# Hybrid decoder step on one core: the place of the constants' small operations and of the first cached-key loads

## The chip, the core and the metric

The kernel runs on one core of a Trainium2 chip. A core has a matrix engine (TensorE, PE in the profile; PEld is its weight load), a vector engine (VectorE, DVE), an engine for activation functions (ScalarE, ACT), a general one (GpSimd, POOL) and an engine that here only starts transfers (SyncE, SP). Each works through its own queue in order; they wait for each other by semaphores. Transfers between the chip's large memory and the core's memory run on 16 DMA engines, started from the queues of SyncE, ScalarE and GpSimd. The metric is the device time of one execution in microseconds. The kernel before took 1861.91 us in the median of three runs (1861.57 to 1862.14).

## The reference

One decoder layer for a prompt of 256 positions and 8 samples of one position each, with the same weights:

```
q, k, v, z, xbc, dt, qm, gates = in_proj(rmsnorm(x))      # one 2048 x 13856 projection
A = sliding-window attention(q, k, v)                     # window 128, ALiBi, sinks
B = SSD scan(xbc, z, dt)                                  # depthwise conv, chunked scan, gated norm
M = cross attention(qm, memory keys, memory values)       # 4 heads of 256, 256 memory tokens
x = x + W_out(g_A * P_A(A) + g_B * P_B(B) + g_M * P_M(M))
x = x + swiglu(rmsnorm(x))
```

For the prompt the memory's keys and values are computed (`w_mem_kv`), for the samples they come from a cache: `cache_mem_k` and `cache_mem_v`, 8 samples x 256 tokens x 1024 values. Everything is fp32; the caches and states are outputs too.

## The kernel before

All features lie along the 128 partitions, and the 264 positions (256 of the prompt and 8 samples) along the columns. The weights are streamed. A **unit** is one block `raw` of 128 x 1024 weights (512 KB), and each unit goes the same way: SyncE loads it (line 261, four buffers); ScalarE rounds it to `hi` (line 183); VectorE takes the rest, `lo = raw - hi` (line 184); TensorE multiplies by `hi` and `lo` (line 162). `hi` and `lo` have three buffers each, so `hi` of unit n waits until TensorE is done with unit n-3, and a block's load waits until VectorE is done with the block four before.

Units 0 to 31 are the memory stage (`mem_group`, accumulators `pmem`): four groups of 8 units, 12 matmuls of 512 columns each; groups 0 and 1 give the keys (norm at line 458), groups 2 and 3 the values. Units 32 to 47 are the projection of the prompt's and samples' memory queries (`qm`, accumulators `pin`), 24 matmuls of 264 columns each, and further groups of `pin` follow; behind them the branches, the output projection and the feed-forward part.

All other work is cut into small steps in generators. `Side.step` runs some of them after each unit, and `side.drain(name)` runs the list up to the end of a named one. The list begins with `mem_norm` ("m"), `prep_x` ("x", the normed activations as `hh` and `hl`: line 578 and the split at lines 183 and 184), `consts` ("c"), `dt_work` ("D"), `mem_keys`, `mem_prompt_work`. The part `consts` makes small tables: slopes and sinks (lines 663 to 675), masks (676 to 679), `na_bc = -exp(a_log)` on 128 x 32 (lines 680 and 681), the same for one column `hcol` (682 and 683), and from the convolution's state, through six transposes, `pre` (lines 688 to 695). Their inputs are loaded by SyncE behind the blocks 17 to 23. `before_q` calls `side.drain("c")` ahead of unit 32. `dt_work` sums `hh` and `hl` to `xf` (line 602).

`mem_prompt_work` squares and transposes the queries; the samples' queries are written to memory as `qd` (line 819, GpSimd's queue). `mem_sample_work` reads each sample's row of `qd` back, broadcast to 128 partitions, as `qb` (line 870), and multiplies it with the cached keys on VectorE (line 875). The cached keys come through `memk_loads` (line 738, GpSimd's queue), a generator that keeps three tiles ahead of the reader.

The order of the instructions on each engine is not the order of the program text: a scheduler at build time puts every instruction where its engine and its inputs are free by its own clock, unless an edge holds it. `tc.issue_after(i)` puts such an edge: each instruction made inside the block stands in its own engine's queue behind `i`, if `i` is on the same engine. It is an order within a queue and no wait for another engine. `state["split_at"]` is the last `hi` that was made (ScalarE), `state["rest_at"]` the last `lo` (VectorE).

Of the kernel before, what the change touches and what calls it, by code (L numbers as in the profile page):

```python
# [79 lines left out]
def tile_hybrid_decoder_step(  # L80
# [9 lines left out]
    nc = tc.nc  # L90
# [9 lines left out]
    side = Side()  # L100
# [7 lines left out]
    def half(name, dt=F32):  # L108
        return ap_.tile([P, 8, NT], dt, tag="A", name=nm(name))

    def t4(name, dt=F32):
        return tp.tile([P, 4 * NT], dt, tag="t4", name=nm(name), bufs=4)
# [4 lines left out]
    def const(shape, name, dt=F32, tag=None):  # L117
        return cp.tile(shape, dt, tag=tag or name, name=name)
# [29 lines left out]
    def t1(name, dt=F32):  # L148
        return tp.tile([P, NT], dt, tag="t1", name=nm(name), bufs=4)

    def tiny(name, n):
        assert n <= 64
        return tp.tile([P, 64], F32, tag="tiny", name=nm(name), bufs=9)[:, 0:n]
# [4 lines left out]
    def sps(name):  # L158
        return pq.tile([P, 512], F32, tag="s", name=nm(name))
# [4 lines left out]
    def tr(out, in_):  # L164
        n = in_.shape[0]
        return nc.tensor.transpose(out, in_, ident[0:n, 0:n])  # L166
# [84 lines left out]
    state = dict(dma=0, split=0)  # L251
# [456 lines left out]
    qt = {}  # L708

    def before_q():  # L710
        side.drain("c")
        qt["qm"] = half("qmT")

    def after_copy(dst):
# [5 lines left out]
    mT = {}  # L720
# [10 lines left out]
    def ahead(sources, pool, depth):  # L731
        tiles = []
        for n in range(len(sources)):
            while len(tiles) < min(n + (depth() if callable(depth) else depth), len(sources)):
                b, src = sources[len(tiles)]
                t = pool("ld")
                for to, of in src(t) if callable(src) else ((t.rearrange("p (b c) -> p b c", b=b) if b else t, src),):
                    nc.gpsimd.dma_start(to, of)
                tiles.append(t)
            yield tiles[n]  # L740
# [8 lines left out]
    def anywhere(name):  # L749
# [3 lines left out]
    memk_loads, memv_loads = (  # L753
        ahead([(None, c[0, b, mc * P:(mc + 1) * P].rearrange("m h d -> m (h d)")) for b in range(NS) for mc in range(2)],
              pool, depth) for c, pool, depth in ((cache_mem_k, anywhere, 3),
                                   (cache_mem_v, values_home, lambda: 3 if ring_free[0] else 2)))
# [15 lines left out]
    def mem_prompt_work():  # L772
# [42 lines left out]
        qrow = t1("qrow")[0:64, 0:P]  # L815
        V.tensor_copy(qrow, p2[0:64, 0:P])
        qd = dr.tile([NS, 1024], F32, name="qd")
        for d in range(2):
            nc.gpsimd.dma_start(qd.rearrange("b (h d c) -> d b h c", h=4, d=2)[d], qrow[32 * d:32 * d + 32])
        mT["qd"] = qd  # L820
        yield 1.5

        for hp in range(2):
            den = tiny("den", 4)
            pT = [t2("pT").rearrange("p (mc t) -> p mc t", mc=2) for _ in range(2)]
            for tb in range(2):
                ps = sps("scm").rearrange("p (h m) -> p h m", h=2)
                for h in range(2):
                    for d in range(2):
                        c = 2 * (2 * hp + h) + d  # L830
# [33 lines left out]
    def mem_sample_work():  # L864
        rq, qd = mT["rq"], mT["qd"]

        sc = const([P, 64], "scs", tag="pTs").rearrange("p (mc b h) -> p mc b h", mc=2, b=NS)
        for b in range(NS):
            qb = t4("qb")[:, 0:1024]
            nc.gpsimd.dma_start(qb, qd[b:b + 1].broadcast_to([P, 1024]))  # L870
            for mc in range(2):
                kc = next(memk_loads)
                jk = t1("jks")
                for h in range(4):
                    V.tensor_tensor_reduce(jk[:, 0:256], kc[:, h * 256:(h + 1) * 256], qb[:, h * 256:(h + 1) * 256],
                                           1.0, 0.0, ALU.mult, ALU.add, sc[:, mc, b, h:h + 1])
                yield 2.0
        ps = sps("sct")
        for mc in range(2):
            tr(ps[0:32, mc * P:(mc + 1) * P], sc[:, mc].rearrange("p b h -> p (b h)"))  # L880
        mx = tiny("mxs", 2)[0:32]
        V.tensor_reduce(mx[:, 0:1], ps[0:32, 0:256], axis=AX.X, op=ALU.max)
        V.tensor_tensor(mx[:, 0:1], mx[:, 0:1], rq[0:32, 17:18], op=ALU.mult)
        pm = t1("pms")[0:32, 0:256]
        act(pm, ps[0:32, 0:256], AF.Exp, scale=rq[0:32, 8:9], bias=mx[:, 0:1], accum_out=mx[:, 1:2])
        V.reciprocal(mx[:, 1:2], mx[:, 1:2])
        V.tensor_scalar(pm, pm, mx[:, 1:2], None, op0=ALU.mult)
        ps = sps("pst")
        for mc in range(2):
            tr(ps[:, mc * 32:(mc + 1) * 32], pm[:, mc * P:(mc + 1) * P])  # L890
        pT = const([P, 64], "pTs")
        V.tensor_copy(pT, ps[:, 0:64])
        mT["p"] = pT
        yield 1.5
# [952 lines left out]
    side.add("D", dt_work(), ["dtw"])  # L1847
    side.add("Km", mem_keys(), ["keys"])
    side.add("Mp", mem_prompt_work(), ["qm"])
    slow.add("Mk", mem_sample_work(), ["q"])  # L1850
    slow.add("Ms", mem_sample_values())
    side.add("W1", swa_keys(), ["kv"])
# [15 lines left out]
    with tc.issue_after(first["load1"].ins):  # L1868
        h = act(warm[:, 0:1], warm[:, 0:1], AF.Copy)
# [65 lines left out]
```

## Time and profile before

| | |
|---|---|
| median of three runs | 1861.91 us |
| the profiled execution's own time | 1862.31 us |
| its span, first to last instruction | 1860.6 us |
| TensorE's granted clock over the span | 1.000 |
| first `pmem` matmul, first `pin` matmul | 8.15 us, 105.91 us |
| VectorE busy from 100 to 110 us, from 110 to 120 us | 10.00 us, 9.39 us |
| DMA, mean over the span | 218 GB/s |

The times in the views are microseconds from the start of the span. The rows of a timeline give the start, the duration, the engine, the line, the operation with its output and inputs and a count; in brackets stands how long the engine was idle before the row, and what it then had waited for. Durations of matmuls overlap, so the distance between two starts tells more than the duration.

### The profile page before, as it was taken

What the parts mean: (1) busy time and instruction counts of PE and PEld (TensorE: products, weight loads), DVE (VectorE), ACT (ScalarE), POOL (GpSimd) and SP (SyncE); (2) the same over time, 40 slices, a digit from 0 to 9 for tenths busy, and PEclk for the clock granted to TensorE, in tenths of its full rate; (3) what the DMA queues carried; (4) which work ended last, traced back from release to release, by engine and by line L of the source; (5) the groups of instructions that cost most, each with busy time, mean ns of one, the idle gap of its engine ahead of it and who ended that gap; (6) DMA issues with size and microseconds to landing.
All of it is one profiled execution on the core that took longest, in us unless ns stands there. A gap on an engine that the chain in (4) does not pass through costs nothing.

```text
span 1860.6 us, 37257 instructions
## 1 busy us (share of the span) xinstructions
PE 1853.2 (100%) x15062; PEld 1810.6 (97%) x15062; DVE 1209.4 (65%) x2355; ACT 953.7 (51%) x1402; POOL 152.7 (8%) x299
## 2 busy tenths in 40 slices
PE   9999999999999999999999999999999999999999
PEld 7789999998999999999999999999999999999999
DVE  6776578776788878887455675555445555445555
ACT  6555466665777676764444444444334443334442
POOL 1100002101011111110000001000000000100001
PEclk9999999999999999999999999999999999999999
DMA  9986669677778777787888767656766556865565
GB/s 282 295 236 201 207 226 300 210 247 235 240 229 264 236 242 243 246 253 241 231 230 253 182 198 219 185 184 179 184 184 183 184 184 180 230 209 182 183 190 150
DMA packets 210265, 406.36 MB, mean 218 GB/s; under 512 B 29487, under 2 KB 34494, under 8 KB 210084
## 3 DMA queue, kind: packets, MB, share of 16 engines
q1 hardware_dynamic: 181508, 323.52, 58.9%
q0 software_dynamic: 21776, 74.15, 12.0%
q10 hardware_dynamic: 6808, 6.30, 1.1%
q8 instruction: 118, 1.93, 0.4%
q14 instruction: 55, 0.45, 0.1%
HBM read 378.38 MB, written 27.81 MB: 218 GB/s over the span
## 4 chain that ended last, share of the span: by engine, by line
PE 61%; DVE 0%; issue 0%; ACT 0%
PE pdn L162 14%; PE pg L162 14%; PE pu L162 14%; PE pin L162 7%; PE pout L162 5%; PE pus L162 5%; PE pua L162 3%; PE py L162 0%; DVE lo L184 0%; PE pst L162 0%; DVE ring L1515 0%; DVE y L1474 0%; PE xtok L166 0%; PE ssy L162 0%; PE yt L166 0%; PE cb L162 0%
## 5 line engine op out<-in xcount | busy, mean ns | idle before, releaser
L184 DVE TENSOR_TENSOR lo<-raw,hi 128x1024 fp32r<-128x1024 f32 (+1 forms) x651 | 747.2, 1153 | 538.4 <-ACT hi L183 535.9
L183 ACT ACTIVATE hi<-raw 128x1024 fp32r<-128x1024 f32 (+1 forms) x651 | 648.1, 1003 | 812.2 <-PE pin L162 184.3
L162 PE MATMUL pin<-hl,hi 128*128 128x264 f32 x1728 | 486.3, 284 | 0.0
L162 PE MATMUL pin<-hh,hi 128*128 128x264 f32 x1728 | 485.5, 284 | 0.0
L162 PE MATMUL pin<-hh,lo 128*128 128x264 f32 x1728 | 474.8, 283 | 0.1
L162 PEld LDWEIGHTS pin<-hl,hi 128*128 128x128 f32 x1728 | 324.2, 188 | 4.2 <-issue 4.0
L162 PEld LDWEIGHTS pin<-hh,hi 128*128 128x128 f32 x1728 | 323.8, 188 | 3.8 <-issue 2.9
L162 PEld LDWEIGHTS pin<-hh,lo 128*128 128x128 f32 x1728 | 318.2, 188 | 3.7 <-issue 3.1
L162 PE MATMUL pu<-h2l,hi 128*128 128x264 f32 x704 | 197.8, 282 | 0.0
L162 PE MATMUL pdn<-fal,hi 128*128 128x264 f32 x704 | 197.7, 282 | 0.0
L162 PE MATMUL pu<-h2h,hi 128*128 128x264 f32 x704 | 197.7, 282 | 0.0
L162 PE MATMUL pg<-h2l,hi 128*128 128x264 f32 x704 | 197.7, 283 | 0.0
L162 PE MATMUL pdn<-fah,hi 128*128 128x264 f32 x704 | 197.3, 282 | 0.0
L162 PE MATMUL pg<-h2h,hi 128*128 128x264 f32 x704 | 197.0, 282 | 0.0
L162 PE MATMUL pdn<-fah,lo 128*128 128x264 f32 x704 | 194.8, 282 | 0.0
L162 PE MATMUL pu<-h2h,lo 128*128 128x264 f32 x704 | 194.7, 282 | 0.0
L162 PE MATMUL pg<-h2h,lo 128*128 128x264 f32 x704 | 194.4, 282 | 0.0
L162 PEld LDWEIGHTS pdn<-fal,hi 128*128 128x128 f32 x704 | 132.0, 188 | 0.0
L162 PEld LDWEIGHTS pg<-h2l,hi 128*128 128x128 f32 x704 | 132.0, 187 | 0.0
L162 PEld LDWEIGHTS pg<-h2h,hi 128*128 128x128 f32 x704 | 132.0, 187 | 0.0
L162 PEld LDWEIGHTS pu<-h2l,hi 128*128 128x128 f32 x704 | 132.0, 187 | 0.0
L162 PEld LDWEIGHTS pu<-h2h,hi 128*128 128x128 f32 x704 | 131.9, 187 | 0.0
(527 smaller groups left out, 2940.4 us busy)
## 6 DMA issues: line engine op xcount, KB each, us to landing
raw<-in_w_in_dram SPq DMA_DIRECT2D x216, 512.0 KB, 4.5
raw<-in_w_gate_dram SPq DMA_DIRECT2D x88, 512.0 KB, 3.6
raw<-in_w_up_dram SPq DMA_DIRECT2D x88, 512.0 KB, 3.5
raw<-in_w_down_dram SPq DMA_DIRECT2D x88, 512.0 KB, 5.0
raw<-in_w_up_ssd_dram SPq DMA_DIRECT2D x32, 512.0 KB, 6.4
raw<-in_w_out_dram SPq DMA_DIRECT2D x32, 512.0 KB, 5.1
raw<-in_w_mem_kv_dram SPq DMA_DIRECT2D x31, 512.0 KB, 6.5
ring<-in_state_ssm_dram POOLq DMA_DIRECT2D x32, 256.0 KB, 5.1
```

The costliest lines, as they stand in the source:

```text
L162: return nc.tensor.matmul(out, lhsT=lhsT, rhs=rhs, start=start, stop=stop)
L183: h = act(hi, src, AF.Copy)
L184: return h, V.tensor_tensor(lo, src, hi.bitcast(F32), op=ALU.subtract)
```

## The change

The instructions of `consts` that are made in `before_q` get their place behind the newest `hi` on ScalarE and behind the newest `lo` on VectorE, which are those of unit 35. That holds for all that the drain runs at that time, so also for the last steps of `prep_x`, the activations. Key loads are placed behind the store of `qd` on GpSimd's queue. Nothing is computed otherwise, and no buffer changes.

```diff
     def before_q():
-        side.drain("c")
+        with tc.issue_after(state["split_at"].ins), tc.issue_after(state["rest_at"].ins):
+            side.drain("c")
         qt["qm"] = half("qmT")
...
         for d in range(2):
-            nc.gpsimd.dma_start(qd.rearrange("b (h d c) -> d b h c", h=4, d=2)[d], qrow[32 * d:32 * d + 32])
+            mT["qd_at"] = nc.gpsimd.dma_start(qd.rearrange("b (h d c) -> d b h c", h=4, d=2)[d], qrow[32 * d:32 * d + 32])
...
             for mc in range(2):
-                kc = next(memk_loads)
+                with tc.issue_after(mT["qd_at"].ins):
+                    kc = next(memk_loads)
```

SyncE's queue is the same as before. On ScalarE the difference begins in the memory stage, at units 15 and 16; `hi_606` and `hi_626` are the `hi` of these units, and line 554 squares the rows of the prompt:

```order
 L183 ACTIVATE hi_606<-raw_581 128x2x512
 L554 ACTIVATE jkx_522,ssx_523<-x_321 128x512 x2
-L680 ACTIVATE na_bc<-na_bc 128x32
 L183 ACTIVATE hi_626<-raw_601 128x2x512
 L554 ACTIVATE jkx_522,ssx_523<-x_483 128x512
```

Line 680 no longer stands ahead of the `hi` of unit 16; line 682, two units further, is gone from there too, and both now stand behind the `hi` of unit 35.

On VectorE the operations of lines 666 to 683 stood around the `lo` of units 15 to 26 (and lines 676 to 679 at the start of the program). The new place is behind `lo_1132`, the `lo` of unit 35; `xn` are the scaled activations:

```order
 L184 TENSOR_TENSOR lo_1132<-raw_1099,hi_1131 128x1024
+L578 SCALAR_TENSOR_TENSOR xn_1135<-xr_550,vgc,rb_924 128x264
+L578 SCALAR_TENSOR_TENSOR xn_1139<-xr_550,vgc,rb_924 128x264
+L666 TENSOR_SCALAR pack<-pack 128x16
+L669 TENSOR_TENSOR m_214_1211<-ident 128x64
+L676 MEMSET pack 128x62
+L679 TENSOR_REDUCE jm<-ident 32x16
+L681 TENSOR_SCALAR na_bc<-na_bc 128x32
+L184 TENSOR_TENSOR hl_123<-xn_1125,hh_121 128x264
+L683 TENSOR_SCALAR hcol<-hcol 32x1
+L693 TENSOR_TENSOR tm_1235<-scT_1231,cw 128x288
```

These rows now stand together there; lines 670, 677 and 678 follow ahead of the `lo` of unit 37, lines 674 and 675 ahead of those of units 38 and 39, and lines 693 and 695 have moved from units 33 and 34 to units 36 and 37. On TensorE the transposes of the convolution's state stand in three places (units 27, 29 and 30) instead of two (28 and 31), and in units 36 to 38 products with `hi` go ahead of those with `lo`.

On GpSimd's queue, before, around the store of `qd` (`ld_` and `ring` are tiles for cached keys, `vm` the prompt's memory values; the other three key loads stand further ahead):

```order
L440 DMA out_dram<-vm_117 128x512 x2
L738 DMA ld_2387<-in_cache_mem_k_dram 128x1024
L440 DMA out_dram<-vm_117 128x512 x2
L655 IOTA ti_1152 128x256
L657 AFFINE_SELECT nd<-nd 128x256
L659 AFFINE_SELECT nd<-nd 128x256
L819 DMA qd<-qrow_1926 32x128 x2
L870 DMA qb_2382<-qd 128x1024
L870 DMA qb_2462<-qd 128x1024
```

And in the changed kernel, whose later lines have numbers higher by one:

```order
L440 DMA out_dram<-vm_117 128x512 x4
L655 IOTA ti_1152 128x256
L657 AFFINE_SELECT nd<-nd 128x256
L659 AFFINE_SELECT nd<-nd 128x256
L820 DMA qd<-qrow_1926 32x128 x2
L739 DMA ld_2384<-in_cache_mem_k_dram 128x1024
L739 DMA ring<-in_cache_mem_k_dram 128x1024
L739 DMA ld_2387<-in_cache_mem_k_dram 128x1024
L739 DMA ring<-in_cache_mem_k_dram 128x1024
L871 DMA qb_2382<-qd 128x1024
```

All four early key loads now stand between the store of `qd` and the four loads of `qb`.

## The prediction

> **What bounds the kernel now.** I read the page's busy table first, then the timeline of TensorE.
>
> ```profile
> span 1860.6 us, 37257 instructions
> PE 1853.2 (100%) x15062; PEld 1810.6 (97%) x15062; DVE 1209.4 (65%) x2355; ACT 953.7 (51%) x1402; POOL 152.7 (8%) x299
> ```
>
> TensorE is busy for the whole span, so only its time counts: work of another engine costs something only where it makes TensorE late. But matmuls overlap, and a busy share of 100% hides short waits. The measure that shows them is the distance between the starts of two matmuls. From the chain of waits, first the undisturbed rate:
>
> ```profile
> 909.99 92.24 PE pus L162 x768
> ```
>
> 768 matmuls in 92.24 us are 0.120 us from start to start for the 264-column ones, with nothing between; the chain runs so from 909.99 us to the last stage. Whatever is lost or won on TensorE before that point therefore moves the end by the same amount: nothing later waits for a fixed time.
>
> Where does TensorE wait? In the memory-key stage (the first 106 us) its matmuls have 512 columns. The timeline of TensorE, columns start, duration, instruction and count, then idle time and its releaser in brackets:
>
> ```profile
> 57.35 0.39 PE L162 MATMUL pmem<-lo,memh 128*128 128x512 f32 x1
> 57.58 0.39 PE L162 MATMUL pmem<-hi,meml 128*128 128x512 f32 x1
> 58.45 0.73 PE L162 MATMUL pmem<-hi,memh 128*128 128x512 f32 x2 [0.48 <-ACT hi L183]
> 59.71 0.50 PE L162 MATMUL pmem<-lo,memh 128*128 128x512 f32 x1 [0.53 <-DVE lo L184]
> 60.05 0.39 PE L162 MATMUL pmem<-hi,meml 128*128 128x512 f32 x1
> ```
>
> 57.35 to 57.58 is the undisturbed distance, 0.23. Then 57.58 to 58.45 is 0.87, too long by 0.64; 58.45 to 59.71 holds two matmuls, 1.26 instead of 0.46, too long by 0.80; 59.71 to 60.05 is too long by 0.11. The **first wait** costs 0.64 + 0.80 + 0.11 = **1.55 us**, of which the brackets show only 1.01. There is one more place:
>
> ```profile
> 73.16 0.62 PE L162 MATMUL pmem<-hi,memh 128*128 128x512 f32 x2
> 74.10 0.50 PE L162 MATMUL pmem<-lo,memh 128*128 128x512 f32 x1 [0.32 <-DVE lo L184]
> 74.43 0.40 PE L162 MATMUL pmem<-hi,meml 128*128 128x512 f32 x1
> ```
>
> 0.94 instead of 0.46 and 0.33 instead of 0.23: the **second wait** costs 0.48 + 0.10 = **0.58 us**. Between 75 us and the last stage the waits of TensorE name no engine at all.
>
> **The constants' operations taken out of the early stage.** What held TensorE at 58 us? ScalarE's timeline before it, and SyncE's issue of the load:
>
> ```profile
> 52.00 0.19 ACT L554 ACTIVATION_READ_ACCUMULATOR jkx<-x 128x1 f32 x1
> 57.22 0.23 ACT L680 ACTIVATE na_bc<-na_bc 128x32 f32<-128x32 f32 x1 [5.04 <-DMA na_bc<-in_a_log_dram]
> 57.36 1.04 ACT L183 ACTIVATE hi<-raw 128x1024 fp32r<-128x1024 f32 x1
> ```
>
> ```profile
> 51.39 0.43 SPq L636 DMA_DIRECT2D na_bc<-in_a_log_dram x1
> ```
>
> ScalarE came to line 680, the exponential of 32 constants, at 52.2 us, and its load had been issued only at 51.39. It stood there for 5.04 us, and behind it in its queue stood the `hi` of unit 16, for which TensorE then waited. VectorE stood twice for the same reason:
>
> ```profile
> 52.76 0.18 DVE L666 TENSOR_SCALAR pack<-pack 128x16 f32<-128x16 f32 x1 [1.08 <-DMA pack<-in_swa_sinks_dram]
> ...
> 57.48 0.18 DVE L681 TENSOR_SCALAR na_bc<-na_bc 128x32 f32<-128x32 f32 x1 [3.34 <-ACT na_bc L680]
> ```
>
> In the changed order lines 666, 680 and 681 stand some 55 us later in the program, behind the split of unit 35, when their loads have long landed. What is late next? The `hi` of unit 16 needs its weight block and a free buffer:
>
> ```profile
> 41.03 2.96 SPq L261 DMA_DIRECT2D raw<-in_w_mem_kv_dram  x2
> ```
>
> ```profile
> raw<-in_w_mem_kv_dram SPq DMA_DIRECT2D x31, 512.0 KB, 6.5
> ```
>
> The block is the second of these two issues, so issued by 44.0; with the median landing of 6.5 us it is there at 50.5. The buffer is that of unit 13, free when TensorE has two units of 12 matmuls (5.5 us) left before 57.81: at 52.3. With 1.04 us for itself `hi` is done at 53.4, 4.4 us before TensorE's turn. So nothing takes the place of the wait: I take all 1.55 us, the other end being 0.
>
> The second wait hangs on VectorE, which TensorE names at 74.10:
>
> ```profile
> 71.25 1.66 DVE L458 SCALAR_TENSOR_TENSOR km<-pmem,rs_y,knm_bc 128x256 f32<-128x256 f32 x4
> 72.83 2.42 DVE L184 TENSOR_TENSOR lo<-raw,hi 128x1024 fp32r<-128x1024 f32 x3
> ```
>
> `lo` of unit 21 starts at 72.83, behind the norm of the keys, which ran late: VectorE was working off what it had missed before 58 us. In the new order it loses 1.08 + 3.34 = 4.42 us less there, while TensorE comes only 1.55 us earlier; lateness of 0.48 us goes away with that. I take the 0.58 us; its ends are 0 and 0.58.
>
> **Their new place.** Behind unit 35's split stand nine small operations (lines 666 to 683) and one `hl` of the activations ahead of `lo` of unit 37 which were not ahead of it before; the two pairs of lines 693 and 695 were there before as well. Units 32 to 39 are where VectorE has no idle time, so this work delays `lo`. The nine are seen at 0.18 and 0.18 above, and the longest is the first row here (the second is an `hl`):
>
> ```profile
> 83.22 0.28 DVE L670 TENSOR_REDUCE m<-m 128x16 f32<-128x64 f32 x1
> ...
> 109.62 0.42 DVE L184 TENSOR_TENSOR hl<-xn,hh 128x264 fp32r<-128x264 f32 x1
> ```
>
> so at most 9 x 0.28 = 2.5 us, by the nearest rows 9 x 0.2 = 1.8, with 0.42 for the `hl`: 2.2 us, at most 2.9. The cover is this:
>
> ```profile
> 114.69 1.06 ACT L183 ACTIVATE hi<-raw 128x1024 fp32r<-128x1024 f32 x1 [1.05 <-PE pin L162]
> ```
>
> ```profile
> 116.07 1.22 DVE L184 TENSOR_TENSOR lo<-raw,hi 128x1024 fp32r<-128x1024 f32 x1
> ```
>
> `hi` of unit 37 starts when TensorE lets go of its buffer, with two units of 24 matmuls still ahead: 48 x 0.120 = 5.8 us, so unit 37's turn is at 120.4. Its `lo` is done at 117.3: 3.1 us to spare, more than 2.9. Cost: 0, if VectorE's full stretch starts as much earlier as TensorE does.
>
> **The key loads.** Four loads of 512 KB leave their early places (before the stores of keys and values) and stand on GpSimd's queue behind the store of the queries `qd` and before the four `qb` loads.
>
> ```profile
> 104.02 0.54 POOL L738 DMA_DIRECT2D ld<-in_cache_mem_k_dram  x1 [18.84 <-PE scT L166]
> ...
> 170.63 1.03 POOL L819 DMA_DIRECT2D qd<-qrow  x2 [47.43 <-DVE rs_y L174]
> 174.24 0.56 POOL L870 DMA_DIRECT2D qb<-qd  x1 [2.58 <-DMA qd<-qrow]
> ```
>
> Four issues take 4 x 0.54 = 2.2 us; `qb` waited 2.58 us for `qd` to land anyway, so its issue stays put. The first reader on VectorE:
>
> ```profile
> 203.75 0.42 DVE L875 CUSTOM_DVE_ANT_0 jks<-ld,qb 128x256 f32<-128x256 f32 x1
> ```
>
> It comes 30 us after the issue. What is added is 2.1 MB on the DMA engines where the 2.1 MB of `qb` already run:
>
> ```profile
> 180.00:190.00 10.00, 10.00 (x81) 9.87 (x80) 6.08 (x15) 4.81 (x13) 0.00 (x0) 1.00 0.82 309
> ```
>
> The last two columns are the DMA share and GB/s: at 0.82, 309 GB/s, so about 377 full. Over 20 us from 172 that is 7.5 MB, against 2.1 + 2.1 of GpSimd and 20/2.9 blocks of 0.52 MB, 3.6 MB: 7.8. Full, but TensorE has several units in hand. Cost: 0, at most the price in the third rival. Taking the loads out early gains nothing by itself, since no wait of TensorE before 106 us but the two above is seen after the start.
>
> **Sum.** 1.55 + 0.58 = 2.13 us. The profiled execution took 1862.31 us (span 1860.6), so 1860.2. The median of the runs, 1861.91, lies 0.4 below it: **1859.8 us**. That is 0.11% faster; a measurement of this kernel can tell about 0.2% from no change, which is 3.7 us, so this is forecast as no change.
>
> **A rule that bears on the waits.** The trace has TensorE's granted clock at 1.00 in every stretch, also around the two waits:
>
> ```profile
> 50.00:60.00 10.00, 8.98 (x38) 6.78 (x37) 5.05 (x14) 4.90 (x12) 1.64 (x3) 1.00 0.79 273
> ```
>
> The Trainium skill, "TensorE: Matmul & The Clock Gate", section "Part 1: The HAM clock gate (the "warmup" mystery)", says that the array falls to half its clock after an idle window of about 3.4 us. By that rule, the trace agrees: idle times of 0.48 and 0.53 us are far too short, and removing them wins no clock besides. An estimate from that page for a new wait of more than 3.4 us would be another 1.7 us or so behind it; the sum has no such wait.
>
> **The rivals.**
> 1. *Only the first wait goes*: VectorE's backlog at 72 us comes from the stage itself. Its whole stretch from 58 us is busy, which speaks for it; the 4.42 us it gets back speak against. 1859.8 + 0.6 = 1860.4. Chance 0.2.
> 2. *VectorE gives it back at unit 37*: its full stretch begins with the activations, behind a `hi` that waited for a weight load:
>
> ```profile
> 92.25 1.06 ACT L183 ACTIVATE hi<-raw 128x1024 fp32r<-128x1024 f32 x1 [2.55 <-DMA raw<-in_w_mem_kv_dram]
> ```
>
> If that load lands at the same time as before while TensorE is 2.1 us earlier, the 3.1 us to spare are 1.0, and 2.2 of added work cost 1.2, at most 1.9: 1861.0, at most 1861.7. Against it: the load is issued when VectorE frees a buffer, which also comes earlier. Chance 0.13.
> 3. *The key loads hold up the weights* between 172 and 195 us, which ends on the slower side. In that stretch the weight blocks of before took to land:
>
> ```profile
> DMA to landing us min/median/max: 3.7/6.5/9.3
> ```
>
> So 2.1 MB of `qb` added up to 5.6 us to the shortest; 4.2 MB would add 11.2 and land a block after 14.9. TensorE can bear about 9.3 plus the 3.1 to spare, 12.4. From there on it decides: a wait of 2.5 us, 1859.8 + 2.5 = 1862.3, slower than before by 0.4. Against it: blocks wait three deep and the rate is not full throughout. Chance 0.06. The Trainium skill, "DMA: Bandwidth & Descriptors", section "Queues, rings and completion order", says that each DMA engine takes turns between the queues packet by packet; by that rule the weights keep half of the rate, an estimated 189 GB/s against the 182 they need, no block is held for the whole of GpSimd's burst, and this rival falls. No run so far shows it for 4.2 MB.
> 4. *The change does not do what it says*: `hi` of unit 16 is late for its own block, and the time stays at 1861.9. The landing at 50.5 speaks against. Chance 0.04.
>
> **How the numbers follow.** Forecast 0.55, rivals 0.2, 0.13, 0.06, 0.04, and 0.02 for a gain above 3.7 us that I don't see. The range takes in the forecast, the first two rivals and their bounds: down to 1858.9, where later waits also shrink a little, and up to 1861.6. Slower by over 0.2% would need more than 5.8 us of new waits on top of what is won: 0.02, out of the third rival. Same: 0.96.
>
> **What would show it.** Right: no idle time of ScalarE before line 680, matmuls 0.23 apart from 57 to 60 and at 73, TensorE's first `pin` at about 103.8 instead of 105.91, and no wait from 110 to 125. Wrong: the first `pin` still near 105.9 (rival 4), at 104.4 (rival 1), gaps before `lo` around 118 to 121 (rival 2), or gaps at 180 to 195 with weight blocks that land after more than 12 us (rival 3).

## The result, and the profile after

| | before | changed |
|---|---|---|
| median of 22 runs each | 1861.95 us (1860.81 to 1863.38) | 1858.93 us (1858.22 to 1859.86) |
| the profiled execution's own time, its span | 1862.31 us, 1860.6 us | 1859.14 us, 1857.3 us |
| ratio, 95% interval | | 0.9983, 0.9977 to 0.9989 |

The kernel became 3.02 us faster where 2.1 were forecast. The forecast called that no change; the interval excludes 1, so it is a gain, a small one. The medians in this document leave out two executions that ran at a granted clock of 0.75 and took 2260 us.

The busy table of the changed kernel, the same line as before: TensorE is still busy throughout.

```profile
PE 1851.2 (100%) x15062; PEld 1810.5 (97%) x15062; DVE 1209.7 (65%) x2355; ACT 953.0 (51%) x1402; POOL 152.2 (8%) x299
```

TensorE's timeline of the changed kernel at the two places where it waited, and its first `pin` matmul (start, duration, instruction, count):

```profile
56.94 0.62 PE L162 MATMUL pmem<-hi,memh 128*128 128x512 f32 x2
57.40 0.39 PE L162 MATMUL pmem<-lo,memh 128*128 128x512 f32 x1
57.63 0.40 PE L162 MATMUL pmem<-hi,meml 128*128 128x512 f32 x1
...
70.72 0.62 PE L162 MATMUL pmem<-hi,memh 128*128 128x512 f32 x2
71.17 0.39 PE L162 MATMUL pmem<-lo,memh 128*128 128x512 f32 x1
71.40 0.40 PE L162 MATMUL pmem<-hi,meml 128*128 128x512 f32 x1
...
102.91 0.28 PE L162 MATMUL pin<-hh,hi 128*128 128x264 f32 x1
```

Two matmuls in 0.46, one in 0.23: both waits are gone. ScalarE's timeline shows the two exponentials at their new place, with no idle time in front:

```profile
106.56 1.06 ACT L183 ACTIVATE hi<-raw 128x1024 fp32r<-128x1024 f32 x1 [0.23 <-ACT hh L183]
107.53 0.21 ACT L680 ACTIVATE na_bc<-na_bc 128x32 f32<-128x32 f32 x1
107.65 0.18 ACT L682 ACTIVATE hcol<-hcol 32x1 f32<-32x1 f32 x1
```

GpSimd's timeline has the key loads behind the store of `qd`, and the windows after them show the DMA engines fuller than before (last columns: DMA share, GB/s):

```profile
166.89 1.03 POOL L820 DMA_DIRECT2D qd<-qrow  x2 [46.82 <-DVE rs_y L174]
167.95 0.55 POOL L739 DMA_DIRECT2D ld<-in_cache_mem_k_dram  x1
...
170.99 0.53 POOL L871 DMA_DIRECT2D qb<-qd  x1 [0.68 <-DMA qd<-qrow]
```

```profile
180.00:190.00 10.00, 10.00 (x73) 9.56 (x72) 4.12 (x9) 4.76 (x11) 0.00 (x0) 1.00 0.87 319
```

Where the time went is read from two rows of each execution that stand at the same work in both, the small matmuls `xn` of the norm ahead of the first wait and behind the second. Before, and then changed:

```profile
48.63 0.29 PE L162 MATMUL xn<-ssx,ones 128*128 128x8 f32 x2
79.81 0.23 PE L162 MATMUL xn<-ssx,sel 128*32 128x8 f32 x2
```

```profile
47.76 0.29 PE L162 MATMUL xn<-ssx,ones 128*128 128x8 f32 x2
76.77 0.23 PE L162 MATMUL xn<-ssx,sel 128*32 128x8 f32 x2
```

The stretch between them is 31.18 us before and 29.01 changed: **2.17 us**, the two waits. The changed execution was 0.87 ahead already at the first of them. From 79.81 to the first `pin` both take the same (26.10 and 26.14). Then there is a place that the prediction has no term for. `pdt` is the product of the summed activations `xf` with the time-step weights (`dt_work`, 16 products of 32 output rows, two records each). TensorE's timeline before, at the last eight of them:

```profile
131.15 0.28 PE L162 MATMUL pin<-hh,lo 128*128 128x264 f32 x1
131.35 0.63 PE L162 MATMUL pdt<-xf,wdt 128*32 128x264 f32 x2
131.92 0.39 PE L162 MATMUL pin<-hh,hi 128*128 128x264 f32 x1
132.15 0.28 PE L162 MATMUL pin<-hl,hi 128*128 128x264 f32 x1
...
134.06 0.28 PE L162 MATMUL pin<-hh,lo 128*128 128x264 f32 x1
134.28 1.09 PE L162 MATMUL pdt<-xf,wdt 128*32 128x264 f32 x14
135.30 0.39 PE L162 MATMUL pin<-hh,hi 128*128 128x264 f32 x1
135.53 0.28 PE L162 MATMUL pin<-hl,hi 128*128 128x264 f32 x1
```

and changed:

```profile
130.31 0.28 PE L162 MATMUL pin<-hh,lo 128*128 128x264 f32 x1
130.52 1.10 PE L162 MATMUL pdt<-xf,wdt 128*32 128x264 f32 x16
131.54 0.39 PE L162 MATMUL pin<-hh,hi 128*128 128x264 f32 x1
131.78 0.28 PE L162 MATMUL pin<-hl,hi 128*128 128x264 f32 x1
```

A place's price is the distance from the last `pin` ahead to the second one behind, less two undisturbed distances of 0.120. Before: 132.15 - 131.15 - 0.24 = 0.76 for one product, 135.53 - 134.06 - 0.24 = 1.23 for seven. Changed: 131.78 - 130.31 - 0.24 = 1.23 for all eight. One product that stood apart cost **0.76 us**; in the changed order it stands with the others.

The last difference is a loss, at the load of `dec` (the decays of the last head group, broadcast to 128 partitions). GpSimd's issue and ScalarE's wait, before and then changed:

```profile
757.69 1.10 POOL L1214 DMA_DIRECT2D dec<-acs_d  x2
...
764.71 2.46 ACT L1419 ACTIVATE dec<-dec,acs_tok 128x128 f32<-128x128 f32 x8 [1.15 <-DMA dec<-acs_d]
```

```profile
753.92 1.09 POOL L1216 DMA_DIRECT2D dec<-acs_d  x2
...
762.08 2.45 ACT L1421 ACTIVATE dec<-dec,acs_tok 128x128 f32<-128x128 f32 x8 [2.28 <-DMA dec<-acs_d]
```

It landed 7.0 us after its issue before, 8.1 changed. Behind it ScalarE copies finished sums out, for which TensorE waited (behind the first group of `pst`, 0.22 us idle, by the profile for ScalarE's `z`); the distance between the two groups of `pst` matmuls there grew from 1.07 to 1.57, so 0.50 was lost. The ledger of the two executions: 0.87 + 2.17 + 0.76 - 0.50 = 3.30, and the spans differ by 3.3. Which of the four belong to the change, and which to the execution, is for the experiments.

### The profile page after: what moved, and what is told of

Same layout as the page of the kernel before. It is cut to its first block, busy times and chain, and to the rows that moved or that the text cites. A ratio compares the mean times of both kernels' runs of the same rounds, so it can differ in the third digit from the quotient of the medians.

```text
span 1857.3 us, 37257 instructions
## 1 busy us (share of the span) xinstructions
PE 1851.2 (100%) x15062; PEld 1810.5 (97%) x15062; DVE 1209.7 (65%) x2355; ACT 953.0 (51%) x1402; POOL 152.2 (8%) x299
## 3 DMA queue, kind: packets, MB, share of 16 engines
q8 instruction: 118, 1.93, 0.4%
## 4 chain that ended last, share of the span: by engine, by line
PE 60%; DMA 1%; DVE 1%; issue 0%; ACT 0%; POOL 0%; POOLq 0%; ACTq 0%
PE pdn L162 14%; PE pg L162 14%; PE pu L162 14%; PE pin L162 6%; PE pout L162 5%; PE pus L162 5%; PE pua L162 3%; DMA dec<-acs_d 0%; DVE lo L184 0%; DMA out_dram<-ring 0%; PE py L162 0%; DVE acc L1226 0%; DVE ring L1517 0%; ACT dec L1421 0%; PE pst L162 0%
```

## The experiments

All times are medians; the ratio is to the kernel before on the same chip (1861.90 to 1862.01 in the three comparisons that follow), in square brackets its 95% interval. Each kernel leaves one profiled execution. Four numbers are read from it as above: the start of the first `xn`; the waits, as the stretch between the `xn` less 29.01; the prices of all places of `pdt` together; the time from issue to landing of the `dec` load, and what TensorE lost by it (distance of the `pst` groups less 1.07).

| kernel | median us, ratio | first `xn` | waits | `pdt` | `dec` lands, lost |
|---|---|---|---|---|---|
| before | 1861.95 | 48.63 | 2.17 | 3.56 | 7.0, 0 |
| before, again | 1861.63, 0.9998 [0.9989, 1.0007] | 47.17 | 1.62 | 3.54 | 7.8, 0.20 |
| before, `pdt` joined | 1861.18, 0.9997 [0.9988, 1.0006] | 47.86 | 2.25 | 2.79 | 8.2, 0.55 |
| key loads alone | 1861.47, 0.9996 [0.9987, 1.0005] | 47.50 | 1.67 | 3.55 | 8.8, 1.14 |
| waiting lines alone | 1860.33, 0.9992 [0.9983, 1.0001] | 48.11 | 0.94 | 3.56 | 8.7, 1.07 |
| constants alone | 1859.38, 0.9987 [0.9979, 0.9996] | 48.72 | 0.27 | 2.81 | 7.9, 0.30 |
| constants alone, again | 1859.02, 0.9982 [0.9973, 0.9991] | 47.83 | 0.12 | 2.79 | 8.2, 0.54 |
| one key load early | 1859.51, 0.9984 [0.9975, 0.9993] | 48.85 | 1.34 | 2.80 | 8.0, 0.35 |
| two key loads early | 1860.37, 0.9992 [0.9983, 1.0001] | 47.72 | 1.77 | 2.79 | 8.3, 0.62 |
| exponential early | 1861.69, 0.9997 [0.9988, 1.0006] | 49.08 | 1.13 | 3.56 | 7.0, 0 |
| changed | 1858.93, 0.9983 [0.9977, 0.9989] | 47.76 | 0.00 | 2.80 | 8.1, 0.50 |
| changed, again | 1858.77, 0.9982 [0.9973, 0.9991] | 47.78 | 0.01 | 2.80 | 7.8, 0.13 |
| `pdt` in one place | 1858.01, 0.9980 [0.9971, 0.9989] | 48.00 | 0.02 | 2.13 | 8.1, 0.47 |
| `pdt` in four whole rounds | 1863.37, 1.0009 [1.0000, 1.0018] | 48.18 | 0.02 | 3.13 | 8.2, 0.55 |

### Each half alone

Constants alone, the first part of the diff and nothing else:

```diff
-        side.drain("c")
+        with tc.issue_after(state["split_at"].ins), tc.issue_after(state["rest_at"].ins): side.drain("c")
```

> The small operations on constants alone are moved, the key loads stay where they were. Theory A (first wait 1.57 us, second wait 0.59, the last 16 pdt records in one run instead of two 0.76, about 0.5 given back later): the same as the changed kernel, 1858.9 us, within 0.3. Rival B (the key loads' leaving their early place brings the part that the waits do not explain, some 0.9 us): 1859.8. The start, if the 0.87 us by which unit 1 was early in the changed kernel's profile comes from lines 676 to 679 no longer standing there: unit 1 at 12.5 us; if it is chance of one execution: anywhere from 12.5 to 13.5.

Measured 1859.38: between theory A and rival B, so the time decides nothing. The trace has the first wait gone, 0.27 us of the second still there, and `pdt` as in the full change. The first matmul of unit 1 starts at 13.52 us, although lines 676 to 679 have left the start of the program as in the full change (12.55): they do not set the start.

Key loads alone, the other two parts of the diff:

```diff
-            nc.gpsimd.dma_start(qd.rearrange("b (h d c) -> d b h c", h=4, d=2)[d], qrow[32 * d:32 * d + 32])
+            mT["qd_at"] = nc.gpsimd.dma_start(qd.rearrange("b (h d c) -> d b h c", h=4, d=2)[d], qrow[32 * d:32 * d + 32])
...
-                kc = next(memk_loads)
+                with tc.issue_after(mT["qd_at"].ins): kc = next(memk_loads)
```

> The key loads alone are moved. Theory A: no change, 1861.9 us within 0.4, the two waits at 58 and 73 us and the two runs of pdt stay. Rival B: 1861.0 or less. Rival C (the loads delay the weight blocks at 172 to 195 us): 1862.3 or more, with gaps of TensorE there. Unit 1 at 13.4 us if lines 676 to 679 set the start.

Measured 1861.47: 0.4 less than before, not to be told from nothing, and less of a gain than rival B asks for. Both waits and the four places of `pdt` stay, and TensorE has no gap at 172 to 195 us: rival C is out. Unit 1 started at 12.30 with lines 676 to 679 at the start, which settles their innocence from the other side. At the `dec` load the execution lost 1.14 us, more than twice what the changed one lost; nothing of this kernel was moved there.

### Only the operations that wait

```diff
-        act(na_bc, na_bc, AF.Exp)
+        with tc.issue_after(state["split_at"].ins), tc.issue_after(state["rest_at"].ins): act(na_bc, na_bc, AF.Exp)
```

and so with lines 666, 681, 682 and 683; the key loads stay early.

> Of the operations on constants only the five with inputs from a load are moved (lines 666, 680 to 683); lines 667 to 679 stay early, and the pdt products stay in their four runs. Theory A: 1861.95 - 2.16 = 1859.8 us, first pin at 103.8. Rival D (what is gained behind the waits belongs to them as well, for instance through buffers that come free earlier): 1858.9. Unit 1 at 13.4 us if lines 676 to 679 set the start, unlike the first run of this set.

Measured 1860.33, slower than either theory said. The first wait is gone, but 0.94 us remain of the second, with VectorE no longer standing at line 666 or 681. Something else makes VectorE late there; the experiments on the early key loads show what.

### The price of an extra place of `pdt`

The kernel before, with the order edge between the products set for all of the second half:

```diff
-                    if q or c:
+                    if q or c or f:
                         tc.keep_in_program_order(m)
```

> Before, with the 16 last pdt records in one run instead of 2 and 14, and one pin product moved as their order asks. Theory A: 0.76 us less, 1861.2. Rival E (a second run of fp32 products costs nothing; the 0.76 us come from the order of the pin products): 1861.95, no change, and unit 44 as far from unit 40 as before, 13.51 us.

Measured 1861.18, as theory A said. The interval doesn't exclude 1, but the trace is sharper: from the first `pin` to the squares of the queries at 165 us this execution takes 0.75 us less than that of before, and the changed one 0.74. These are the ends of the stretch, before (its first `pin` is at 105.91), here, and changed (first `pin` at 102.91):

```profile
165.63 0.64 PE L162 MATMUL ssq<-sqm,ones 128*32 128x256 f32 x8
```

```profile
105.17 0.28 PE L162 MATMUL pin<-hh,hi 128*128 128x264 f32 x1
164.14 0.64 PE L162 MATMUL ssq<-sqm,ones 128*32 128x256 f32 x8
```

```profile
161.89 0.64 PE L162 MATMUL ssq<-sqm,ones 128*32 128x256 f32 x8
```

59.72, 58.97 and 58.98 us. The constants are at their old place in this kernel, so the term is shown apart from them, and rival E is out.

### The changed kernel, the constants alone and the kernel before, once more

> The changed kernel a second time, for its spread. Theory F (the start and the first load of dec near 764 us are chance of one execution; the two waits, the pdt run and the key loads are the change): from 48 to 80 us TensorE is 2.2 us less late than before within 0.2, from the first pin to 165 us 0.74 less; the start anywhere from 0.9 earlier to 0.1 later than in the profile of before; TensorE loses 0 to 1.2 us at the dec load, by how long the load takes beyond some 7.5 us. Median 1858.9. If the start belongs to the change it is again 0.87 earlier.

> The constants alone a second time, beside the full change on one chip. Theory F: weight blocks still land late behind the third key load at 52.6 us (over 8 us from issue), so TensorE keeps 0.1 to 0.6 us of the second wait; 0.3 to 0.6 us slower than the full change, 1859.4. Rival (the key loads do nothing): the same as the full change within 0.2.

> Before a second time, for its spread. Theory F: both waits again (1.2 to 1.6 and 0.5 to 1.0 us), four runs of pdt; unit 1 anywhere from 12.3 to 13.5 us, TensorE loses 0 to 1.2 us at the dec load, where the first profile of before had lost nothing. 1861.9. If the start belongs to the change, unit 1 is again at 13.4.

Measured 1858.77, 1859.02 and 1861.63. The kernel before started its second execution earlier than any other kernel here (47.17), so the 0.87 us at the start were an execution's chance. Its waits came to 1.62, somewhat under what was expected of them: the first was only 0.58 us, the second 0.97. The constants alone stayed 0.25 us behind the full change, a little less than expected, with 0.12 us of the second wait left: for or against the key loads this says little.

The load of `dec` is chance too, and follows one line over all fourteen executions: TensorE loses nothing if it lands after 7.0 us, 0.13 to 0.20 at 7.8, 0.30 at 7.9, 0.35 at 8.0, 0.47 and 0.50 at 8.1, 0.54 and 0.55 at 8.2, 0.62 at 8.3, 1.07 and 1.14 at 8.7 and 8.8. The first execution of before had one of the two shortest landings.

### The early key loads

The changed kernel with one of the four loads left free (its place is the old one, between the stores of keys at 51 us and at 71):

```diff
-                    nc.gpsimd.dma_start(to, of)
+                    with tc.issue_after(mT["qd_at"].ins) if pool is anywhere and tiles else nullcontext(): nc.gpsimd.dma_start(to, of)
```

> The changed kernel with the first of its key loads back at its early place, between the two stores of keys at 51 us and those at 68; the other three stay behind qd. Theory F: as the constants alone, weight blocks land up to 8 us or more after issue at 55 to 72 us, ScalarE waits for them, TensorE loses 0.1 to 0.6 us at 70 to 72 us; 1859.3. Rival G (the two key loads at 22 and 30 us do it, since they delay everything behind them): as the full change, 1858.9, and no wait of TensorE at 70.

Measured 1859.51, 0.7 more than the full change in the same comparison, and 1.34 us of waits; rival G is out. Then two of them, right behind one another:

```diff
-  with tc.issue_after(mT["qd_at"].ins) if pool is anywhere and tiles else nullcontext():
+  with tc.issue_after(mT["qd_at"].ins) if pool is anywhere and len(tiles) > 1 else tc.issue_after(mT["k0"].ins) if pool is anywhere and tiles else nullcontext():
```

> The changed kernel with two of its four key loads back behind the first stores of keys, at about 51 us, one right behind the other (1 MB). Theory F (a key load that runs while the weight blocks of units 18 to 23 are under way makes them late): blocks land up to 9 us or more after their issue, TensorE loses 0.5 to 1.5 us between 68 and 74 us, 1859.4 to 1860.4. Rival (the 1.34 us lost in the run with one of them there was chance, and TensorE has enough in hand): nothing lost, 1858.9.

Measured 1860.37, 1.4 to 1.6 more than the two medians of the full change, and 1.77 us of waits; theory F. ScalarE and VectorE with two early loads (of `raw` the last row gives the time to landing between 20 and 76 us):

```profile
57.48 1.14 ACT L183 ACTIVATE hi<-raw 128x512 fp32r<-128x512 f32 x2
61.80 0.32 ACTq L522 DMA_DIRECT2D x<-in_x_prompt_dram  x1
62.16 0.47 ACT L449 ACTIVATE jk<-pmem,rs_m 128x256 f32<-128x256 f32 x1 [3.54 <-DMA raw<-in_w_mem_kv_dram]
```

```profile
63.35 0.17 DVE L451 TENSOR_SCALAR ssk<-ssk 128x4 f32<-128x4 f32 x1 [3.92 <-ACT jk L449]
```

```profile
71.05 0.62 PE L162 MATMUL pmem<-hi,memh 128*128 128x512 f32 x2
72.79 0.50 PE L162 MATMUL pmem<-lo,memh 128*128 128x512 f32 x1 [1.12 <-DVE lo L184]
```

```profile
DMA to landing us min/median/max: 4.9/6.4/9.8
```

and the same work in the changed kernel:

```profile
57.52 1.14 ACT L183 ACTIVATE hi<-raw 128x512 fp32r<-128x512 f32 x2
58.30 0.32 ACTq L522 DMA_DIRECT2D x<-in_x_prompt_dram  x1
58.67 0.47 ACT L449 ACTIVATE jk<-pmem,rs_m 128x256 f32<-128x256 f32 x1
```

```profile
DMA to landing us min/median/max: 4.1/6.3/7.2
```

The chain is this. With two key loads in flight the weight block issued at 51.98 us landed 9.8 us later, at 61.8; in the changed kernel the one issued at 51.99 took 6.3 us, to 58.3. In both, ScalarE's load of `x` went out just then (61.80, 58.30), and behind it in the queue stood the squares `jk` of the finished keys. Why this load waits for that block no run shows. VectorE waited 3.92 us for the squares, its norm of the keys ran late and with it `lo`, and TensorE lost 1.28 us at 71.05 (1.74 instead of 0.46).

All nine executions in which line 680 stands late follow one line here. Counted from the first `xn`, this load of `x` goes out after 10.5 and 11.0 us in the two executions of the changed kernel and after 12.2 in the two with `pdt` moved, and these lose 0.00 to 0.02 us. After 12.4, 12.6, 13.2, 13.6 and 14.1 us (constants alone again, constants alone, waiting lines alone, one key load, two key loads) TensorE loses 0.12, 0.27, 0.94, 1.34 and 1.77: whatever goes beyond some 12.3 us is lost in full. So this chain is also what the waiting lines alone left behind.

That the key loads make the block late is shown less sharply. The load of `x` goes out 6.3, 6.7, 8.0 and 8.0 us after the block's issue without an early key load, 7.8, 8.3, 8.7 and 9.4 with one at 52 us (three of these kernels have the other three early as well), and 9.8 with two. For two loads the time of the runs says the same; for one, the medians differ by 0.25 to 0.74 us. With line 680 at its early place, the kernel before included, the same block landed after 5.8 to 6.8 us, and this chain is not seen.

### The exponential alone, back at its early place

```diff
     def consts():
+        es = ExitStack(); es.enter_context(tc.issue_after(state["split_at"].ins)); es.enter_context(tc.issue_after(state["rest_at"].ins))
...
-        act(na_bc, na_bc, AF.Exp)
+        es.close(); act(na_bc, na_bc, AF.Exp)
...
-        act(hcol[:, 1:2], hcol[:, 1:2], AF.Exp)
+        es = ExitStack(); es.enter_context(tc.issue_after(state["split_at"].ins)); es.enter_context(tc.issue_after(state["rest_at"].ins)); act(hcol[:, 1:2], hcol[:, 1:2], AF.Exp)
```

and a close at the end of `consts`, in place of the edges around the drain.

> The changed kernel with only lines 680 and 681 (exponential and sign of na_bc) back at their early place; the order of the pdt products falls back to four places with it. Theory F: ScalarE waits again some 5 us for the load of na_bc, TensorE loses 1.1 to 1.6 us at 56 to 59 us, and because VectorE stands some 3 us at line 681, 0.3 to 0.6 at 71 to 73; the pdt products 0.74 more: 1858.9 + 2.2 to 2.9 = 1861.1 to 1861.8. Rival H (the second wait comes from the other small operations, or from line 666): no wait at 71 to 73, 1860.7 to 1861.2.

Measured 1861.69, inside the range of theory F; rival H is out. ScalarE waited 4.11 us there. TensorE lost 0.49 us at 73 us, as expected, and at 58 us 0.61, which is less than the expected 1.1 to 1.6. So the backlog behind line 681 does bring on the second wait as well: either cause is enough.

### Fewer and more places

The changed kernel with all four sums `xf` first, and the products in reverse order, so that the first of them needs the last sum:

```diff
-        for f in range(2):
-            full = []
+        full = []
+        for f in range(2):
...
-            yield None
-            for q in range(2):
+        yield None
+        for f in (1, 0):
+            for q in (1, 0):
...
-                           start=f == q == 0, stop=f == q == 1)
-                    if q or c:
+                           start=f == q == 1, stop=f == q == 0)
+                    if not (f and q) or c:
```

> The changed kernel with all 16 pdt products in one place instead of three (their sum in the reverse order). Theory R: two places less, 2 x 0.34 = 0.68 us less from first pin to 165 us, 1858.2, faster than both kernels. Rival P: 2 x 0.74 = 1.5 less, 1857.4. Rival: VectorE's four sums now stand in a row before it and make lo late, 1858.9 or more.

Measured 1858.01, 0.8 to 0.9 less than the two medians of the full change and faster than both kernels. TensorE's timeline at the one place:

```profile
128.97 0.28 PE L162 MATMUL pin<-hh,lo 128*128 128x264 f32 x1
129.18 2.00 PE L162 MATMUL pdt<-xf,wdt 128*32 128x264 f32 x32
131.11 0.39 PE L162 MATMUL pin<-hh,hi 128*128 128x264 f32 x1
131.34 0.28 PE L162 MATMUL pin<-hl,hi 128*128 128x264 f32 x1
```

131.34 - 128.97 - 0.24 = 2.13, against 2.80 in three places: theory R to 0.01.

The last eight products in two places of four:

```diff
+                if q: yield None
                 for c in range(4):
...
-                    if q or c:
+                    if c:
```

> The changed kernel with its last eight pdt products in two places, four and four, instead of one place. Each product writes 32 rows of the result, four of them beside one another. Theory R (a place costs 0.34 us for going over and back, and each round of four products 0.44): from first pin to 165 us 0.34 more than the changed kernel, 1859.2. Rival P (what the change saved, 0.74, is the price of a place): 0.74 more, 1859.7.

Measured 1863.37, far off both theories. From the first `pin` to the squares of the queries the execution takes 0.80 us more than the changed one, which would be rival P's number. But 472 records of `pin` stand in this stretch instead of 468, and 4 x 0.120 = 0.48 of the 0.80 are theirs. The four places themselves cost 3.13 us, 0.33 more than the three, as theory R says (0.34) and rival P does not (0.74); and to the first transpose of the keys, further on, the execution takes 0.37 more.

The new step in `dt_work` also gave the scheduler another order for everything behind it, and from the squares to the first product of the output projection (485 us in the changed kernel) the execution lost another 3.2 us. No two neighbouring `pin` stand too far apart there; the other work's places among `pin` cost more, 63.14 us against 59.14 from the first `pin` on, and these 4.00 are all of it: 0.33 + 0.48 + 3.2. At 410 us, for instance, the products `oms`, of 32 output rows as well, stand in three pieces between transposes, and the place costs 3.88 us; in the changed kernel eight records of `oms` in one place cost 1.19 to 1.28. So TensorE's order decided here too, but the time of the whole kernel says nothing about `pdt`.

## Where the prediction was right, and which step failed

**The first wait** (1.55 us) and **the second** (0.58 us). Right in sum: 2.13 forecast, 2.17 measured between the same rows of the two executions; over the three executions of the kernel with the constants and key loads early the waits were 2.17, 1.62 and 2.25, so 2.0. The split was that of one execution: in the other two the first wait was 0.58 and 1.19, the second 0.97 and 1.01. That the sum came out to 0.04 is in part luck. Nothing took the place of the waits. The first `pin` was forecast at 103.8 and came at 102.91, and the difference is the start's 0.87.

**The cause of the second wait** was half right. The prediction put it on VectorE's backlog from lines 666 and 681 and said of the key loads: "Taking the loads out early gains nothing by itself". For the key loads alone the runs do not contradict that (0.4 us, inside the interval). But with the waiting lines moved and the key loads early 0.94 us of waits remained, with all constants moved 0.12 to 1.34; it takes both to be rid of it. Its first rival (backlog of the stage itself) was right in that there is a second source, and wrong in what it is. The key loads' share is 0.2 to 0.7 us by the medians, no more exactly than that.

**The new place of the constants** cost nothing, as forecast: TensorE had no wait from 110 to 125, and the second rival is out.

**The key loads behind `qd`** cost nothing. `qb` still waited 0.68 us for `qd` after the four issues, and from the squares of the queries to the first transpose of the keys TensorE takes 77.00 us before and 76.98 changed. Weight blocks issued from 168 to 198 us landed within 9.8 us, against 9.3 before and the 14.9 of the third rival, which fell although the stretch ran at a DMA share of 0.87. By the Trainium skill, "DMA: Bandwidth & Descriptors", section "Queues, rings and completion order", which the prediction cited for the turns between the queues, that was to be expected; the trace agrees in the result.

**The sum** is the step that failed. "1.55 + 0.58 = 2.13" has terms for ScalarE, VectorE and the queues, and none for TensorE's own order, although TensorE bounds the kernel and the account of the change names differences in its order. One product of `pdt` that no longer stood alone is worth 0.76 us: 2.13 + 0.76 = 2.89, against 3.02 measured; with the mean of 2.0 for the waits it is 2.8. The rest, 0.1 to 0.3 us, is hardly above what these runs resolve (the standard deviation of single runs is 0.6 us before and 0.4 changed, so some 0.16 for the difference of two sets of 22). The start and the `dec` load, which are also in the ledger of the two executions, are chance, and nearly cancel.

**The bound for "no change"** was too coarse as well. The prediction took 0.2%; with 22 runs of each kernel the half interval is 0.06%, so even the 2.13 us, 0.11%, would have been told from none.

Why a product apart costs so much: each `pdt` product fills 32 of the 128 output rows. A place with one product takes 0.57 us from its start to the next `pin`, one with four 0.58, with seven or eight 1.02, with sixteen 1.93. So four of them run beside one another and a round of up to four costs 0.44; going over and back costs the remaining 0.34. The price 0.34 + 0.44 n for n rounds gives 0.78, 1.22 and 2.10, measured 0.78, 1.23 and 2.13. Before, one product had a place and a round to itself; changed, neither. The Trainium skill, "TensorEngine Tiling (Array Packing)", section "Tiling Modes", says that different tiles can work in parallel and that changing the tiling mode drains TensorE; by that, both terms are what one must expect, and the trace agrees and gives the prices.

## What to carry to other kernels

Where an engine is busy for the whole span, every difference in its own order has to be priced, also the ones that nobody meant: count the places at which narrow products interrupt wide ones, and the rounds of four in each. A small operation on a loaded constant costs little on its engine, but in an in-order queue it holds everything behind it until the load is there, and prefetches taken too early can do the same by making the weights late. Before a difference between two profiled executions is put down to a change, look at the same rows in several executions of each kernel: here two of four differences were chance, 0.87 and 0.50 us, and the causes 0.58 to 1.55.

## What the runs showed of the hardware

The matmuls of 512 columns at the very start run 0.43 us apart and then 0.23, and when they change over differs between executions of almost the same program. Before, and then with the key loads alone:

```profile
12.14 0.62 PE L162 MATMUL pmem<-hi,meml 128*128 128x512 f32 x1
12.57 0.42 PE L162 MATMUL pmem<-lo,memh 128*128 128x512 f32 x1
12.83 0.39 PE L162 MATMUL pmem<-hi,meml 128*128 128x512 f32 x1
```

```profile
9.53 0.50 PE L162 MATMUL pmem<-lo,memh 128*128 128x512 f32 x1
9.87 0.39 PE L162 MATMUL pmem<-hi,meml 128*128 128x512 f32 x1
10.09 0.39 PE L162 MATMUL pmem<-lo,memh 128*128 128x512 f32 x1
```

Over fourteen executions the first `pmem` matmul started between 7.40 and 8.53 us and the first `xn` matmul between 47.17 and 49.08 us, whatever was changed, while the window from 8 to 12 us shows a granted clock of 1.00 in both. The Trainium skill, "TensorE: Matmul & The Clock Gate", section "Part 1: The HAM clock gate (the "warmup" mystery)", says that the clock goes up at the end of a free-running window of about 3.4 us, so that the moment varies from run to run; the distances of the matmuls agree with that, the clock column does not show it.

A load of one row broadcast to 128 partitions (`dec`) took 7.0 to 8.8 us from issue to landing in executions that do the same there, and with some 7.7 us at hand, by the line of losses above, TensorE's end moves with it. A good part of the spread from run to run, 2.6 us before and 1.6 changed between the fastest and the slowest, will have these two sources; that is argued from the profiles, not shown for the runs without one.
